# Seven block products for 25 of 32 column-block pairs of the SwiGLU input products, with the sums of weight blocks on GpSimd

## The chip, the core and the metric

The kernel runs on one core of one Trainium2 chip, in one launch. The metric is device time in microseconds; the figure is the median of three runs. All matrices are float32, and TensorE multiplies them as float32r parts: each factor is split into a high part (rounded to float32r) and a low part (what is left), and a product is the sum of three: high by high, low by high, high by low.

## The reference, cut to what matters

256 tokens of 2048 features pass through two layers of three sublayers each. Four of the six sublayers are SwiGLU feed-forward blocks with 4096 hidden features:

```
def swiglu(x, w_in, w_out):                  # x: 256 x 2048, w_in: 2048 x 8192, w_out: 4096 x 2048
    a, gate = jnp.split(x @ w_in, 2, axis=-1)
    return (jax.nn.silu(a) * gate) @ w_out

x = layer_norm(ALPHA * x + 0.5 * swiglu(x, w_in, w_out), g, b)
```

The other two are a stick-breaking attention and a causal pooling mixer. The product `x @ w_in` is what the change is about. Cut into 512 columns, w_in has 8 blocks for `a` and 8 for `gate`; a column-block pair is block n of `a` with block n of `gate`, and there are 8 pairs in each feed-forward block, 32 in all.

## The kernel before

The residual stream lies with features on the partitions: 16 tiles (`xf`) of 128 features by 256 tokens, and beside each its high and low float32r parts (`xs`), side by side.

Weights come from device memory by SyncE's queue in chunks (`chunk`, line 118): four 128-row tiles of 512 columns, 1 MB, into one of three `raw` buffers. For each half of a chunk ScalarE casts the high part into a `whi` tile (line 133) and VectorE subtracts it from the raw weights for the low part, into a `wlo` tile (line 134). Both pools have five tiles of 128x1024.

A product (`gemm`, line 139) goes through the weights a column block at a time. The weights are the stationary operand, 128 columns at a time, and the tokens move: for each 128x128 block of weights the high part meets the 512 columns of [high | low] of x (line 157), the low part meets the 256 columns of the high part (line 160). A column block has 16 row tiles and four 128-column parts, so 64 such couples of products, in four PSUM banks. ScalarE copies the right half of a bank out and VectorE adds the left half (`total`, lines 194 and 195); then come SiLU, the multiplication with the gate (line 334) and the split of the result into parts (line 101).

`ffn_in` (line 319) runs the eight pairs one after the other, `a` block first, then the gate block. In three of the four feed-forward blocks the first pair (in one of them the first two) is computed ahead of the layer norm (`ahead`): x is scaled by the gain only, two columns more carry gain and bias, and all three products go into one sum of 258 columns (lines 151 to 153). Meanwhile the layer norm is finished. GpSimd has nothing to do in these products; it makes constants at the start, takes seven small powers for the layer norms (line 201), and issues eight DMAs at the end.

The last sublayer ends by token: for its output product the tokens are the stationary operand, 128 at a time, and 512 columns of weights move (lines 572 to 574).

The instructions of each engine stand in a fixed order that a scheduler chose when the program was built; an engine starts an instruction when all that stand ahead of it on its queue have been started and its semaphores are there.

Of the kernel before, what the change touches and what calls it, by code (L numbers as in the profile page):

```python
# [13 lines left out]
P = 128  # L14
T = 256
# [20 lines left out]
def trunk(ctx: ExitStack, tc: tile.TileContext, a: dict, out: bass.AP):  # L36
# [4 lines left out]
    whis = ctx.enter_context(tc.tile_pool(name="whis", bufs=5))  # L41
    wlos = ctx.enter_context(tc.tile_pool(name="wlos", bufs=5))
# [24 lines left out]
    # The tensor engine runs at its full clock only after a while of work: products for  # L67
    # nothing, until the first data is here.
# [7 lines left out]
    # tri[k', k] = 1 where k' >= k; past[k, q] = 1 where k < q, twice.  # L76
# [20 lines left out]

    def split(dst, hi_src, lo_src):
# [18 lines left out]
    def chunk(w, r, c, fine=False, step=4):  # L117
        """Four 128-row tiles of 512 columns of w, in halves of hi and lo parts."""
        raw = raws.tile([P, 4, 512], F32, tag="raw", name="raw")
        if fine:  # L120
            for j in range(4):
                load_x(0, j)
                nc.sync.dma_start(raw[:, j], w[r, c, :, j])
        else:
            for j in range(0, 4, step):
                nc.sync.dma_start(raw[:, j:j + step], w[r, c, :, j:j + step])
        his, los = [], []
        for j in range(2):
            hi = whis.tile([P, 2, 512], F32R, tag="whi", name="whi")
            lo = wlos.tile([P, 2, 512], F32R, tag="wlo", name="wlo")  # L130
            for i in ((slice(0, 1), slice(1, 2)) if step < 4 else (slice(0, 2),)):
                src = raw[:, 2 * j:2 * j + 2][:, i]
                nc.scalar.copy(hi[:, i], src)  # L133
                nc.vector.tensor_tensor(out=lo[:, i], in0=src, in1=hi[:, i].bitcast(F32), op=ALU.subtract)  # L134
            his += [hi[:, i] for i in range(2)]
            los += [lo[:, i] for i in range(2)]
        return his, los

    def gemm(w, col, rhs, evac, hooks=None, load=False, one=0, r0=0):
        """Four 128-row tiles of (a 512-column block of w).T @ x, one bank each: hi*hi + lo*hi left,  # L140
        hi*lo right; or all in one sum of that many columns."""
# [41 lines left out]
    def total(dst, ps, norm=None):  # L183
        """dst = left + right half of a product; or, of a raw one, what the layer norm makes of it,
        but for the bias that is returned."""
        if norm is not None:
            aux = tmp.tile([P, 2], F32, tag="aux", bufs=4, name="aux")
            nc.scalar.copy(aux, ps[:, T:W])
            nc.vector.scalar_tensor_tensor(out=dst, in0=norm.rb[:, T:], scalar=aux[:, 0:1], in1=ps[:, :T],
                                           op0=ALU.mult, op1=ALU.add)  # L190
            nc.vector.tensor_tensor(out=dst, in0=dst, in1=norm.rb[:, :T], op=ALU.mult)
            return aux[:, 1:2]
        t = tmp.tile([P, T], F32, tag="half", name="half")
        nc.scalar.copy(t, ps[:, T:])  # L194
        nc.vector.tensor_tensor(out=dst, in0=ps[:, :T], in1=t, op=ALU.add)  # L195

# [9 lines left out]
    class Norm:  # L206
        """LN of what x holds, less a shift: its statistics, 1 / std and -mean on all partitions,
        and its result, for four tiles at a time. Ahead of it, xs = [hi | lo] of gain * x."""
# [12 lines left out]
        def add(self, t):  # L221
            """Tiles t and t + 1."""
            q, j = divmod(t, 4)
            x, s = xq[q][:, j:j + 2].rearrange("p j n -> p (j n)"), self.sums
            if t == 0:
                nc.scalar.copy(s[:, 0], x)
                nc.scalar.activation(s[:, 1], x, AF.Square)
            else:
                sq = tmp.tile([P, 2 * T], F32, tag="sq", name="sq")
# [3 lines left out]
            gx = tmp.tile([P, 2, T], F32, tag="gx", name="gx")  # L233
# [37 lines left out]
    def sublayer_end(w, rhs, factor, gname, bname, hooks=None, one=0):  # L271
        """x <- LN(ALPHA x + factor y): LN of x + (factor / ALPHA) y, with eps / ALPHA**2."""
# [43 lines left out]
    def ffn_in(w_in, norm, hooks=None, npairs=1):  # L316
        gs = [None] * (FF // P)
        for grp in range(FF // 512):
            acts = []
            nm = norm if grp < npairs else None  # L320

            def evac_a(f, ps, acts=acts, nm=nm):
                s = tmp.tile([P, T], F32, tag=f"act{f}", bufs=1, name="act")
# [4 lines left out]
            def evac_gate(f, ps, grp=grp, acts=acts, nm=nm):  # L328
                t = 4 * grp + f
                gs[t] = scratch(t, F32R, f"g{t}").rearrange("p (h n) -> p h n", h=2)  # L330
                g = tmp.tile([P, T], F32, tag="gate", name="gate")
                bias = total(g, ps, nm)
                if bias is None:
                    nc.vector.tensor_tensor(out=g, in0=g, in1=acts[f], op=ALU.mult)
                else:
                    nc.vector.scalar_tensor_tensor(out=g, in0=g, scalar=bias, in1=acts[f], op0=ALU.add, op1=ALU.mult)
                split(gs[t], g, g)

            ca, cg = (w_in, grp, evac_a), (w_in, FF // 512 + grp, evac_gate)
            if nm is not None:  # L340
                ahead(nm, (ca, cg), first=grp == 0, last=grp == npairs - 1)
            else:
                gemm(*ca[:2], whole, ca[2], hooks=(hooks or {}).get(grp), load=grp == 0 and norm is None)
                gemm(*cg[:2], whole, cg[2])
        return gs

    def ffn(p, i, ln, norm, npairs=1):
        gs = ffn_in(a[f'{p}ffn{i}_w_in'], norm, npairs=npairs)
# [5 lines left out]
    def attention(p, norm):  # L354
# [17 lines left out]
        def diag(x):  # L372
            """The two blocks where only some of the keys are past."""
            return x.rearrange("p (j q) -> p j q", j=3)[:, ::2]

        def scores(hg):
            def go():
                hs = range(4 * hg, 4 * hg + 4)
                with tc.manual_schedule(engines={mybir.EngineType.Activation}):
                    for h in hs:  # L380
                        # By key: keys 0..127 for all queries, keys 128..255 for the later queries.
# [8 lines left out]
                    # One table after the other.  # L390
# [4 lines left out]
                for h in hs:  # L395
                    # softplus(z) of the past keys
# [5 lines left out]
        def weights(hg):  # L402
            def go():
# [7 lines left out]
                for h in hs:  # L411
                    # exp(min(log_w, 0))
# [41 lines left out]
    def pooling(p, norm):  # L454
# [3 lines left out]
        gates = {}  # L458

        def evac_u(grp, nm):  # L460
            def evac(f, ps):
# [11 lines left out]
                q = tmp.tile([P, T], F32, tag="sq", name="q")  # L473
# [6 lines left out]
        def evac_g(grp, nm):  # L480
            def evac(f, ps):
                s = tmp.tile([P, T], F32, tag=f"act{f}", bufs=1, name="act")
# [29 lines left out]
    def last(p, norm):  # L512
# [16 lines left out]
        gs = ffn_in(w_in, norm, hooks={2: {0: turn}})  # L529
# [65 lines left out]
    norm = ffn('l0_', 2, 'ln3', norm, npairs=2)  # L595
# [32 lines left out]
```

## Time and profile before

| | |
|---|---|
| Time, median of 3 runs (lowest, highest) | 2683.83 us (2683.7, 2683.9) |
| The profiled execution: span, first to last instruction | 2681.8 us |
| The profiled execution's own time, its span and the 2.0 us by which the median run is longer | 2683.8 us |
| TensorE busy | 2666.7 us (99%) |
| VectorE busy | 1675.7 us (62%) |
| ScalarE busy | 1365.4 us (51%) |
| GpSimd busy | 11.9 us (0%) |
| Granted TensorE clock, mean | 0.998 |
| One plain column-block pair | 44.92 us |

A busy time is the time in which at least one instruction of the engine runs; the mean of one instruction can be longer than its share, since the engines are pipelined and neighbours overlap. What an instruction costs in a row of them is read from the distance of two starts.

### The profile page before, as it was taken

How to read it: one execution, taken by the hardware profiler on the slowest of the kernel's cores; microseconds unless marked ns; L12 is line 12 of the kernel's file. 1: busy time of each engine (PE TensorE's matmuls, PEld its weight loads, DVE VectorE, ACT ScalarE, POOL GpSimd, SP SyncE). 2: the span in 40 equal slices, each digit the busy share in tenths (PEclk: the TensorE clock that was granted, in tenths of full speed). 3: DMA queues.
4: the chain of work that ended last, by engine and by line, in shares of the span. 5: the costliest groups of instructions: out<-in, count | busy, mean ns of one | idle time of the engine just before them, and what ended most of it. 6: DMA issues, size and time to landing. Idle time of an engine off the chain costs nothing.

```text
span 2681.8 us, 38727 instructions
## 1 busy us (share of the span) xinstructions
PE 2666.7 (99%) x15916; PEld 2365.1 (88%) x15916; DVE 1675.7 (62%) x2298; ACT 1365.4 (51%) x1990; POOL 11.9 (0%) x28
## 2 busy tenths in 40 slices
PE   9999999999999999999999999999999999999998
PEld 8888888899999888888988888889888998888886
DVE  6555556585686555565765555667878775555545
ACT  5444444467565444444654444445555565444432
POOL 0000000000000000000000000000000000000000
PEclk9999999999999999999999999999999999999999
DMA  7555555554455555555555555554555545555653
GB/s 255 188 188 187 189 188 189 189 174 162 153 190 183 187 186 186 199 177 201 173 189 189 189 189 189 189 189 170 192 189 176 201 174 182 186 186 187 228 193 126
DMA packets 71521, 499.61 MB, mean 186 GB/s; under 512 B 7984, under 2 KB 8624, under 8 KB 12080
## 3 DMA queue, kind: packets, MB, share of 16 engines
q1 hardware_dynamic: 70704, 495.05, 52.4%
q8 instruction: 124, 2.03, 0.3%
q0 software_dynamic: 640, 2.10, 0.2%
q14 instruction: 53, 0.43, 0.0%
HBM read 495.02 MB, written 2.10 MB: 185 GB/s over the span
## 4 chain that ended last, share of the span: by engine, by line
PE 99%; DVE 1%; DMA 0%; SPq 0%; ACT 0%; issue 0%; DVEq 0%; ACTq 0%
PE ps L157 50%; PE ps L160 26%; PE ps L152 5%; PE ps L151 5%; PE ps L153 5%; PE y L573 2%; PE y L572 2%; PE y L574 2%; PE v L430 1%; PE v L428 1%; PE v L429 1%; DMA xq<-in_x 0%; PE cum L407 0%; DVE z L547 0%; PE bc L257 0%; PE st L244 0%
## 5 line engine op out<-in xcount | busy, mean ns | idle before, releaser
L134 DVE TENSOR_TENSOR wlo<-raw,whi 128x1024 fp32r<-128x1024 f32 (+1 forms) x946 | 1144.3, 1212 | 905.8 <-ACT whi L133 901.2
L133 ACT CAST whi<-raw 128x1024 fp32r<-128x1024 f32 (+1 forms) x946 | 982.0, 1041 | 1080.1 <-PE ps L157 851.9
L157 PE MATMUL ps<-xs,whi 128*128 128x512 f32 x3968 | 1389.8, 396 | 1.1 <-ACT whi L133 0.7
L160 PE MATMUL ps<-xs,wlo 128*128 128x256 f32 x3968 | 1100.5, 280 | 1.0 <-DVE wlo L134 1.0
L157 PEld LDWEIGHTS ps<-xs,whi 128*128 128x128 f32 x3968 | 744.8, 189 | 173.4 <-ACT whi L133 1.0
L160 PEld LDWEIGHTS ps<-xs,wlo 128*128 128x128 f32 x3968 | 748.3, 189 | 7.3 <-DVE wlo L134 1.5
L157 PE MATMUL ps<-g,whi 128*128 128x512 f32 x1536 | 534.9, 394 | 0.0
L160 PE MATMUL ps<-g,wlo 128*128 128x256 f32 x1536 | 427.8, 280 | 0.0
L157 PEld LDWEIGHTS ps<-g,whi 128*128 128x128 f32 x1536 | 287.2, 187 | 65.3
L160 PEld LDWEIGHTS ps<-g,wlo 128*128 128x128 f32 x1536 | 289.7, 189 | 1.1
L152 PE MATMUL ps<-xs,whi 128*128 128x258 f32 (+1 forms) x896 | 252.7, 284 | 0.0
L151 PE MATMUL ps<-xs,whi 128*128 128x258 f32 (+1 forms) x896 | 251.7, 283 | 0.0
L153 PE MATMUL ps<-xs,wlo 128*128 128x258 f32 (+1 forms) x896 | 245.5, 282 | 0.0
L152 PEld LDWEIGHTS ps<-xs,whi 128*128 128x128 f32 x896 | 169.6, 189 | 0.2
L151 PEld LDWEIGHTS ps<-xs,whi 128*128 128x128 f32 x896 | 168.9, 188 | 0.0
L153 PEld LDWEIGHTS ps<-xs,wlo 128*128 128x128 f32 x896 | 167.6, 190 | 0.0
L194 ACT COPY half<-ps 128x256 f32<-128x256 f32 x264 | 97.1, 369 | 121.0 <-PE ps L157 119.6
L572 PE MATMUL y<-wlo,g 128*128 128x512 f32 x256 | 99.6, 389 | 0.0
L573 PE MATMUL y<-whi,g 128*128 128x512 f32 x256 | 99.6, 389 | 0.0
L574 PE MATMUL y<-whi,g 128*128 128x512 f32 x256 | 99.4, 389 | 0.0
L157 PE MATMUL ps<-y,whi 128*128 128x512 f32 x256 | 89.6, 396 | 0.0
L195 DVE TENSOR_TENSOR act<-ps,half 128x256 f32<-128x256 f32 x124 | 52.1, 421 | 46.6 <-ACT half L194 46.6
(151 smaller groups left out, 1677.0 us busy)
## 6 DMA issues: line engine op xcount, KB each, us to landing
raw<-in_l_ffn_w_in SPq DMA_DIRECT2D x252, 1024.0 KB, 4.8
raw<-in_l_ffn_w_out SPq DMA_DIRECT2D x127, 1024.0 KB, 4.8
raw<-in_l_pool_w_in SPq DMA_DIRECT2D x32, 1024.0 KB, 4.9
raw<-in_l_sb_w_qkv SPq DMA_DIRECT2D x24, 1024.0 KB, 4.8
raw<-in_l_pool_w_out SPq DMA_DIRECT2D x16, 1024.0 KB, 4.9
raw<-in_l_sb_w_o SPq DMA_DIRECT2D x8, 1024.0 KB, 4.9
raw<-in_l_pool_w_grp SPq DMA_DIRECT2D x4, 1024.0 KB, 4.9
raw<-in_l_ffn_w_in SPq DMA_DIRECT2D x6, 512.0 KB, 9.4
```

The lines of the kernel that those rows point to most:

```text
L133: nc.scalar.copy(hi[:, i], src)
L134: nc.vector.tensor_tensor(out=lo[:, i], in0=src, in1=hi[:, i].bitcast(F32), op=ALU.subtract)
L151: nc.tensor.matmul(ps[:, :one], hi[:, cs], x[:, 0, :one], start=first, stop=False)
L152: nc.tensor.matmul(ps[:, :one], hi[:, cs], x[:, 1, :one], start=False, stop=False)
L153: nc.tensor.matmul(ps[:, :one], lo[:, cs], x[:, 0, :one], start=False, stop=last)
L157: nc.tensor.matmul(ps.rearrange("p (h n) -> p h n", h=2), hi[:, cs], x, start=first, stop=last)
L160: nc.tensor.matmul(ps[:, :T], lo[:, cs], x[:, 0], start=False, stop=False)
L194: nc.scalar.copy(t, ps[:, T:])
L195: nc.vector.tensor_tensor(out=dst, in0=ps[:, :T], in1=t, op=ALU.add)
L572: nc.tensor.matmul(ps[m], gh, lo, start=kk == 0, stop=False)
L573: nc.tensor.matmul(ps[m], gl, hi, start=False, stop=False)
L574: nc.tensor.matmul(ps[m], gh, hi, start=False, stop=kk == nk - 1)
```

## The change

A column-block pair becomes one 2x2 block product. The tokens are cut into two blocks of 128 and the 2048 features into two of 1024, so x is [A11 A12; A21 A22]; the weights of the pair are [B11 B12; B21 B22], where the first index is the half of the features and the second is `a` or `gate`. Eight block products of 128 tokens by 1024 features by 512 columns are replaced by seven (Winograd's form of Strassen's product). The four sums of x blocks are made once per feed-forward block on GpSimd (`prepare`). The four sums of weight blocks are made for each 128 features of both halves, eight times in a pair, on GpSimd (`ta`: B12-B11 and B12-B22; `tb`: B22 less the first of these, and B21 less that). High and low parts of B11, of B21 and B22, of `ta` and of `tb` are then made on ScalarE and VectorE as before. In the seven products the tokens are stationary and 512 columns of weights move.

25 of the 32 pairs go this way. In the first feed-forward block the first pair stays as it was. In the other three the first pair is computed ahead of the layer norm as before, and the second by a plain product with the tokens stationary (`gemm_x`). In the feed-forward block that had two pairs ahead of the layer norm, one is left.

The results of the pairs by `gemm_x` and by seven products lie by token. They are multiplied, turned by TensorE's transposes to lie by feature, kept in float32 (`whole_pair`), and split into parts later (`settle`): eight tiles within the last pair, 24 behind it. Buffers: `whi` and `wlo` have six tiles, two tiles for the sums are new, and several small tiles share a pool (`wide`). The host lays out the weights of the 25 pairs by blocks; it adds nothing up.

```
+    sums = ctx.enter_context(tc.tile_pool(name="sums", bufs=2))
-    whis = ctx.enter_context(tc.tile_pool(name="whis", bufs=5))
-    wlos = ctx.enter_context(tc.tile_pool(name="wlos", bufs=5))
+    whis = ctx.enter_context(tc.tile_pool(name="whis", bufs=6))
+    wlos = ctx.enter_context(tc.tile_pool(name="wlos", bufs=6))
...
+    def gemm_x(w, col, rhs):
...
+                for m in range(2):
+                    xh, xl = (rhs[kk][:, h, m * P:(m + 1) * P] for h in range(2))
+                    nc.tensor.matmul(ps[m], xh, his[k], start=kk == 0, stop=False)
+                    nc.tensor.matmul(ps[m], xl, his[k], start=False, stop=False)
+                    nc.tensor.matmul(ps[m], xh, los[k], start=False, stop=kk == nk - 1)
+        return ps
+    class Seven:
...
+        def prepare(self, q):
+            a11, a21 = (xq[q][:, :, m * P:(m + 1) * P] for m in range(2))
+            a12, a22 = (xq[q + 2][:, :, m * P:(m + 1) * P] for m in range(2))
+            t = [wide(f"s{i}").rearrange("p (j n) -> p j n", j=4) for i in range(4)]
+            for dst, x, y, op in ((t[0], a21, a22, ALU.add), (t[1], t[0], a11, ALU.subtract),
+                                  (t[3], a12, t[1], ALU.subtract), (t[2], a21, a11, ALU.subtract)):
+                nc.gpsimd.tensor_tensor(out=dst, in0=x, in1=y, op=op)
...
+        def run(self, w, grp, hooks):
...
+            for i in range(8):
+                raw = raws.tile([P, 4, 512], F32, tag="raw", name="raw")
+                nc.sync.dma_start(raw, w[grp, i])
+                b11, b2, b22, b21 = raw[:, 1], raw[:, 2:4], raw[:, 3], raw[:, 2]
+                def parts(hi, lo, src):
+                    nc.scalar.copy(hi, src)
+                    nc.vector.tensor_tensor(out=lo, in0=src, in1=hi.bitcast(F32), op=ALU.subtract)
...
+                ta, tb = (sums.tile([P, 2, 512], F32, tag="sum", name=n) for n in ("ta", "tb"))
+                nc.gpsimd.tensor_tensor(out=ta, in0=raw[:, 0:1].to_broadcast([P, 2, 512]), in1=raw[:, 1:4:2],
+                                        op=ALU.subtract)
+                nc.gpsimd.tensor_tensor(out=tb[:, 0], in0=b22, in1=ta[:, 0], op=ALU.subtract)
+                nc.gpsimd.tensor_tensor(out=tb[:, 1], in0=b21, in1=tb[:, 0], op=ALU.subtract)
...
+                parts(h11, l11, b11)
+                hb, lb = pair()
+                parts(hb, lb, b2)
+                ha, la = pair()
+                parts(ha, la, ta)
+                ht, lt = pair()
+                parts(ht, lt, tb)
...
+                for n in ((1, 2, 6, 5, 3, 7, 4) if i == 7 else products):
+                    (xh, xl), hi, lo = products[n]
...
+                    nc.tensor.matmul(p, xh, hi, start=i == 0, stop=False)
+                    nc.tensor.matmul(p, xl, hi, start=False, stop=False)
+                    nc.tensor.matmul(p, xh, lo, start=False, stop=i == 7)
...
+            nc.scalar.copy(s1, p1)
+            add(c11, p2, s1)
+            add(u2, p6, s1)
+            add(u4, p5, u2)
+            add(c12, p3, u4)
+            add(c22, p7, u4)
+            add(u2, p7, u2)
+            add(c21, p4, u2)
+            return (c11, c21), (c12, c22)
...
+        def settle(ts):
+            for t in ts:
...
+                split(gs[t], src, src)
...
+        def gated(grp, a, g):
+            for m in range(2):
+                nc.vector.tensor_tensor(out=a[m], in0=a[m], in1=g[m], op=ALU.mult)
...
+                            nc.tensor.transpose(ps[:, j * T + m * P:j * T + (m + 1) * P], a[m][:, f * P:(f + 1) * P],
+                                                ident)
+                    nc.scalar.copy(whole_pair(2 * grp + h), ps)
...
+        seven.prepare(0)
+        seven.prepare(1)
+        late = None
+        for grp in range(1, std):
+            pa = gemm_x(w_in, grp, xs)
...
+        for grp in range(std, ng):
+            hs = {1: late} if late else {}
+            if grp == ng - 1:
+                hs[5] = lambda: settle(range(8))
+            acts, gates = seven.run(w_seven, grp - std, hs)
+            late = gated(grp, silu(acts, acts), gates)
+        late()
+        settle(range(8, 32))
         return gs
```

What this makes of the engines' queues is seen at two places. The first is GpSimd's queue. Before, this is all that it holds between the start of the program and its end: a counter and two masks, five powers of a variance (`var`), and at the end the DMAs of a gain (`gb`).

```order
L88 IOTA count_115 128x16
L79 AFFINE_SELECT tri_107<-tri_107 128x128
L85 AFFINE_SELECT past_112<-past_112 128x256
L201 TENSOR_TENSOR rn_4979<-var_4983,mhalf_105 128x2
L201 TENSOR_TENSOR rn_7104<-var_7108,mhalf_105 128x2
...
L534 DMA gb0_23347<-in_l1_ln3_g 128x512 x4
```

Now, in the middle of the pairs by seven products of the first feed-forward block, it stands like this (`raw` is the chunk of weights, `ta` and `tb` the sums):

```order
L379 TENSOR_TENSOR tb_842<-raw_839,ta_841 128x512
L380 TENSOR_TENSOR tb_842<-raw_839,tb_842 128x512
L377 TENSOR_TENSOR ta_883<-raw_881 128x1024
L379 TENSOR_TENSOR tb_884<-raw_881,ta_883 128x512
L380 TENSOR_TENSOR tb_884<-raw_881,tb_884 128x512
L377 TENSOR_TENSOR ta_927<-raw_925 128x1024
L379 TENSOR_TENSOR tb_928<-raw_925,ta_927 128x512
L380 TENSOR_TENSOR tb_928<-raw_925,tb_928 128x512
```

Three subtractions of weight blocks for each 1 MB of weights are added, 600 in all, and 32 sums of x blocks beside them; the powers stay.

The second place is VectorE's queue within the first feed-forward block. Before, around the evacuation of a gate block (`ps`, `half`), it holds the low parts of the weights, two for each chunk, and the small tiles of the activations:

```order
L134 TENSOR_TENSOR wlo_1372<-raw_1369,whi_1371 128x1024
L134 TENSOR_TENSOR wlo_1376<-raw_1369,whi_1375 128x1024
L134 TENSOR_TENSOR wlo_1418<-raw_1415,whi_1417 128x1024
L195 TENSOR_TENSOR gate_1314<-ps0_1175,half_1315 128x256
L334 TENSOR_TENSOR gate_1314<-gate_1314,act_1121 128x256
L195 TENSOR_TENSOR gate_1330<-ps1_1176,half_1331 128x256
L334 TENSOR_TENSOR gate_1330<-gate_1330,act_1134 128x256
L101 TENSOR_TENSOR g8_1313<-gate_1314,g8_1313 128x256
```

Now, at the end of a pair by seven products (`p2`, `p6`: PSUM banks of two of the products; `su` and `c11`: sums of products; `half` and `act` are gone):

```order
L369 TENSOR_TENSOR wlo_2042<-raw_2030,whi_2041 128x1024
L369 TENSOR_TENSOR wlo_2038<-raw_2074,whi_2037 128x512
L369 TENSOR_TENSOR wlo_2046<-ta_2032,whi_2045 128x1024
L369 TENSOR_TENSOR wlo_2050<-tb_2033,whi_2049 128x1024
L369 TENSOR_TENSOR wlo_2084<-raw_2074,whi_2083 128x1024
L418 TENSOR_TENSOR c11_2118<-p2_1778,su_2116 128x512
L369 TENSOR_TENSOR wlo_2088<-ta_2076,whi_2087 128x1024
L369 TENSOR_TENSOR wlo_2092<-tb_2077,whi_2091 128x1024
L369 TENSOR_TENSOR wlo_2142<-raw_2134,whi_2141 128x512
L369 TENSOR_TENSOR wlo_2146<-raw_2134,whi_2145 128x1024
L418 TENSOR_TENSOR su_2116<-p6_1794,su_2116 128x512
```

For each 1 MB of weights VectorE now holds three and a half subtractions of 1024 elements instead of two, half of their elements made by GpSimd (`ta`, `tb`), and the sums of products stand between those of the next pair's first weights (`raw_2134`).

## Rows read from the trace of the kernel before

**Rows 1.** The page: busy us of each engine, share of the span, instructions.

```profile
PE 2666.7 (99%) x15916; PEld 2365.1 (88%) x15916; DVE 1675.7 (62%) x2298; ACT 1365.4 (51%) x1990; POOL 11.9 (0%) x28
```

**Rows 2.** The page: the chain that ended last, shares of the span by engine.

```profile
PE 99%; DVE 1%; DMA 0%; SPq 0%; ACT 0%; issue 0%; DVEq 0%; ACTq 0%
```

**Rows 3.** Windows: a plain pair; 192 matmuls by token of the last output product.

```profile
core 0: us, PE busy (x) PEld busy (x) DVE busy (x) ACT busy (x) POOL busy (x), PEclk, DMA share, GB/s
1385.12:1430.04 44.92, 44.92 (x258) 39.20 (x257) 25.37 (x34) 22.12 (x33) 0.00 (x0) 1.00 0.53 187
2538.90:2582.30 43.40, 43.40 (x194) 35.92 (x193) 22.09 (x20) 16.76 (x17) 0.00 (x0) 1.00 0.55 194
```

**Rows 4.** Waits of the whole run: in total, times, longest.

```profile
engine line waited for: us in total, times, longest us
DVE wlo L134 <- ACT whi L133: 901.2, 667, 5.1
ACT whi L133 <- PE ps L157: 851.9, 562, 4.2
```

**Rows 5.** Timeline, VectorE: low parts back to back (us of the start, us).

```profile
start us, us, engine line op out<-in xcount [idle before <-releaser]
14.02 2.56 DVE L134 TENSOR_TENSOR wlo<-raw,whi 128x512 fp32r<-128x512 f32 x4
27.77 2.36 DVE L134 TENSOR_TENSOR wlo<-raw,whi 128x1024 fp32r<-128x1024 f32 x2 [3.08 <-ACT whi L133]
```

**Rows 6.** Groups by form, VectorE: names, shapes, count, busy us, mean ns.

```profile
L134 DVE TENSOR_TENSOR wlo<-raw,whi 128x1024 fp32r<-128x1024 f32 x926 | 1131.2, 1223 | 898.9 <-ACT whi L133 894.6
L588 DVE SCALAR_TENSOR_TENSOR z<-y,z 128x512 f32<-128x512 f32 x8 | 5.5, 687 | 6.5 <-PE y L574 6.5
L101 DVE TENSOR_TENSOR g<-gate,g 128x256 fp32r<-128x256 f32 x128 | 53.0, 418 | 0.0
```

**Rows 7.** Groups by form, ScalarE: the high parts.

```profile
L133 ACT CAST whi<-raw 128x1024 fp32r<-128x1024 f32 x926 | 970.4, 1050 | 1071.9 <-PE ps L157 851.9 <-PE y L574 93.8 <-PE ps L152 91.8
```

**Rows 8.** Groups by form, GpSimd: the powers and two masks.

```profile
L201 POOL TENSOR_TENSOR rn<-var,mhalf 128x2 f32<-128x2 f32 x5 | 3.5, 695 | 2138.4 <-DVE var L251 2138.4
L201 POOL TENSOR_TENSOR rs<-ve,mhalf 128x1 f32<-128x1 f32 x2 | 1.9, 968 | 184.8 <-DVE ve L542 184.8
L85 POOL TENSOR_SCALAR_AFFINE_SELECT past<-past 128x256 f32<-128x256 f32 x1 | 0.4, 396 | 0.0
L79 POOL TENSOR_SCALAR_AFFINE_SELECT tri<-tri 128x128 f32<-128x128 f32 x1 | 0.3, 282 | 0.0
```

**Rows 9.** Timeline, GpSimd: one of five early powers, and the last two.

```profile
561.57 0.71 POOL L201 TENSOR_TENSOR rn<-var,mhalf 128x2 f32<-128x2 f32 x1 [558.94 <-DVE var L251]
2665.69 1.00 POOL L201 TENSOR_TENSOR rs<-ve,mhalf 128x1 f32<-128x1 f32 x1 [178.67 <-DVE ve L542]
2672.85 0.93 POOL L201 TENSOR_TENSOR rs<-ve,mhalf 128x1 f32<-128x1 f32 x1 [6.16 <-DVE ve L542]
```

**Rows 10.** Timeline, VectorE: beside these three powers.

```profile
561.33 0.15 DVE L251 SCALAR_TENSOR_TENSOR var<-st,m 128x2 f32<-128x2 f32 x1
563.98 1.23 DVE L134 TENSOR_TENSOR wlo<-raw,whi 128x1024 fp32r<-128x1024 f32 x1 [2.50 <-ACT whi L133]
2665.52 1.41 DVE L547 SCALAR_TENSOR_TENSOR z<-z,mv,gb 128x512 f32<-128x512 f32 x2
2666.84 0.75 DVE L552 SCALAR_TENSOR_TENSOR z<-z,rs,gb 128x512 f32<-128x512 f32 x1
2672.63 1.40 DVE L547 SCALAR_TENSOR_TENSOR z<-z,mv,gb 128x512 f32<-128x512 f32 x2
2673.95 0.74 DVE L552 SCALAR_TENSOR_TENSOR z<-z,rs,gb 128x512 f32<-128x512 f32 x1
```

**Rows 11.** The page: DMA issues of input weights, median us to landing.

```profile
raw<-in_l_ffn_w_in SPq DMA_DIRECT2D x252, 1024.0 KB, 4.8
```

**Rows 12.** The chain in order of time: eight 128-column float32 matmuls.

```profile
565.85 0.89 PE bc L257 x8
```

More of the change, by code (lines that the diff above doesn't have):

```diff
@@ L96, in vec, with wide @@
         return vecs[:, c:c + 1]
+    def wide(name):
+        return tmp.tile([P, 512], F32, tag="wide", bufs=4, name=name)
     def split(dst, hi_src, lo_src):
@@ L313, in ahead @@
             gemm(w, col, xs, evac, hooks=hooks, one=W)
-    def ffn_in(w_in, norm, hooks=None, npairs=1):
-        gs = [None] * (FF // P)
[L318 to L323, printed above, removed]
+    def gemm_x(w, col, rhs):
+        nk = len(rhs)
+        ps = [bank(f"px{m}") for m in range(2)]
+        for c in range(nk // 4):
+            his, los = chunk(w, c, col)
+            for k in range(4):
+                kk = 4 * c + k
+                for m in range(2):
[4 more added lines that the diff above has]
+        return ps
@@ new lines, in ffn_in, with whole_pair, silu, go @@
+    def ffn_in(w_in, w_seven, norm, hooks=None):
+        ng = FF // 512
+        ahead_of = 0 if norm is None else 1
+        std = ahead_of + 1 if norm is not None else 1
+        g32 = [None] * (FF // P // 2)
+        gs = [None] * (FF // P)
+        seven = Seven()
+        def whole_pair(i):
+            g32[i] = scratch(i, F32, f"gw{i}")
+            return g32[i]
+        def settle(ts):
+            for t in ts:
+                slot = 16 + t if t < 16 else 32 if t == 31 else t - 16
+                gs[t] = scratch(slot, F32R, f"g{t}").rearrange("p (h n) -> p h n", h=2)
+                src = g32[t // 2][:, t % 2 * T:(t % 2 + 1) * T]
+                split(gs[t], src, src)
+        def silu(a, src):
+            for m in range(2):
+                nc.scalar.activation(a[m], src[m], AF.Silu)
+            return a
+        def gated(grp, a, g):
+            for m in range(2):
+                nc.vector.tensor_tensor(out=a[m], in0=a[m], in1=g[m], op=ALU.mult)
+            def go():
+                for h in range(2):
+                    ps = bank("gt")
+                    for j in range(2):
+                        f = 2 * h + j
+                        for m in range(2):
+                            nc.tensor.transpose(ps[:, j * T + m * P:j * T + (m + 1) * P], a[m][:, f * P:(f + 1) * P],
+                                                ident)
+                    nc.scalar.copy(whole_pair(2 * grp + h), ps)
+            return go
+        def by_feature(grp):
+            acts, pairs = [], []
+            nm = norm
+            def evac_a(f, ps):
+                if f % 2 == 0:
+                    pairs.append(wide("act"))
+                s = pairs[-1][:, f % 2 * T:(f % 2 + 1) * T]
@@ L333, in evac_gate @@
                 if bias is None:
-                    nc.vector.tensor_tensor(out=g, in0=g, in1=acts[f], op=ALU.mult)
+                    nc.vector.tensor_tensor(out=dst, in0=g, in1=acts[f], op=ALU.mult)
                 else:
[L336 to L344, printed above, removed]
@@ L345, in ffn_in @@
-        return gs
-    def ffn(p, i, ln, norm, npairs=1):
-        gs = ffn_in(a[f'{p}ffn{i}_w_in'], norm, npairs=npairs)
+                    nc.vector.scalar_tensor_tensor(out=dst, in0=g, scalar=bias, in1=acts[f], op0=ALU.add, op1=ALU.mult)
+            return (w_in, 0, evac_a), (w_in, std, evac_gate)
+        ca, cg = by_feature(0)
+        if norm is not None:
+            ahead(norm, (ca, cg))
+        else:
+            gemm(*ca[:2], whole, ca[2], load=True)
+            gemm(*cg[:2], whole, cg[2])
@@ new lines, in ffn_in @@
+        seven.prepare(0)
[3 more added lines that the diff above has]
+            pa = gemm_x(w_in, grp, xs)
+            acts = silu([wide(f"a{m}") for m in range(2)], pa)
+            if hooks:
+                hooks()
+            late = gated(grp, acts, gemm_x(w_in, std + grp, xs))
+        for grp in range(std, ng):
[4 more added lines that the diff above has]
+            late = gated(grp, silu(acts, acts), gates)
@@ L349, in ffn @@
+        late()
+        settle(range(8, 32))
+        return gs
+    def ffn(p, i, ln, norm):
+        gs = ffn_in(a[f'{p}ffn{i}_w_in'], a[f'{p}ffn{i}_w_in_seven'], norm)
         if norm is None:
@@ L457, in pooling @@
                       for i, n in enumerate(("y", "po")))
-        gates = {}
+        gates, pairs = {}, []
         def evac_u(grp, nm):
@@ L527, in turn @@
                     nc.scalar.copy(z[q][:, m, :], ps[m])
-        gs = ffn_in(w_in, norm, hooks={2: {0: turn}})
+        gs = ffn_in(w_in, a[f'{p}ffn2_w_in_seven'], norm, hooks=turn)
         for i, name in enumerate((f'{p}ln3_g', f'{p}ln3_b')):
@@ L594, in trunk @@
     norm = attention('l0_', norm)
-    norm = ffn('l0_', 2, 'ln3', norm, npairs=2)
+    norm = ffn('l0_', 2, 'ln3', norm)
     norm = ffn('l1_', 1, 'ln1', norm)
@@ L614 @@
             value = value[0].T.reshape(4, 4, P, T).transpose(0, 2, 1, 3)
+        elif name.endswith('_w_in') and '_ffn' in name:
+            std = 1 if name == 'l0_ffn1_w_in' else 2
+            blocks = value.reshape(2, 8, P, 2, 8, 512)
+            laid[name + '_seven'] = np.stack(
+                [blocks[h, :, :, n, std:] for h, n in ((0, 1), (0, 0), (1, 0), (1, 1))]).transpose(3, 1, 2, 0, 4)
+            value = blocks[:, :, :, :, :std].reshape(4, 4, P, 2 * std, 512).transpose(0, 3, 2, 1, 4)
         elif '_w_' in name:
```

57 lines of the change are left out of this document (49 added, 8 removed).

## The prediction

> **What bounds the kernel now.** I read the page's busy times first: TensorE 99%, VectorE 62%, ScalarE 51%, GpSimd nothing [rows 1]. The chain that ended last says the same, 99% TensorE [rows 2]. Then windows over one column-block pair: it takes 44.92 us, TensorE is busy in all of it at the full granted clock, and VectorE in 25.37 us, ScalarE in 22.12 us [rows 3]. The waits confirm the direction: VectorE's low parts wait for ScalarE's high parts, and those for TensorE to give buffers back [rows 4]. So the input products are bound by TensorE, and work taken from it is worth its time until another engine becomes the limit. The question is which engine comes next, since the change takes a little from TensorE and gives much to VectorE and GpSimd.
>
> **TensorE's part.** A pair had 128 products of 512 columns and 128 of 256 in 44.92 us. By seven products it has 7 x 8 x 3 = 168 of 512 columns with the tokens stationary. The last output product is of that form: 192 in 43.40 us, so 0.226 us each [rows 3]. 168 x 0.226 = 38.0 us, and eight transposes of 128 columns at 0.89 / 8 = 0.11 us [rows 12] make 38.9 us. TensorE alone would give back 6.0 us for each of 25 pairs, 150 us. Each of the three pairs by `gemm_x` is 192 such products, 43.4 instead of 44.9 us (taking a pair ahead of the norm at the plain price): 5 us together.
>
> **VectorE's part.** In a pair there are eight steps of 1 MB. In each the low parts are three subtractions of 1024 elements and one of 512 where there were two of 1024. Back to back, four of 512 took 2.56 us and two of 1024 took 2.36 [rows 5]; less one whole duration (0.69 for a VectorE operation on 512 and 1.22, [rows 6]) that is a distance of 0.62 and 1.14 us. A step is 3 x 1.14 + 0.62 = 4.04 us, eight are 32.3. At the pair's end come seven sums from PSUM and two gate products of 512, 9 x 0.62 = 5.6 us; together 37.9 us, just under TensorE. ScalarE's 1024-element cast is 1.05 us [rows 7]: three and a half in a step, 8 x 3.7 = 29.4 us, not a limit.
>
> **GpSimd's part.** A step adds one subtraction of 1024 and two of 512, in a chain: `tb` needs `ta`, its second half needs its first. No row of before shows a GpSimd operation on two large inputs. The nearest are the masks with one input, 0.282 us for 128 elements and 0.396 for 256 [rows 8]: 0.89 ns an element and 0.17 us fixed. If two inputs cost no more than one, a step's 2048 elements cost 2048 x 0.89 + 3 x 0.17 = 2.3 us; if two reads and a write each cost that in turn, 6.0 us. I take two reads, 4.15 us. Alone, beside the others, that is 33 us a pair and hidden.
>
> [...]
>
> **Whether the two run side by side.** This decides the sign. All of VectorE's low parts read two tensors from SBUF, and so does every one of the new GpSimd instructions. The trace has seven small GpSimd operations with two inputs. The five powers for the layer norms fell where VectorE was idle: at 561.57 us VectorE had just ended at 561.48 and next started at 563.98. They took 0.695 us in the mean. The two at the end started 0.17 and 0.22 us after a VectorE operation with two SBUF inputs (line 547) and took 1.00 and 0.93 us, with fewer elements [rows 8 to 10]. The first of each couple on line 547 gives way to the second 0.66 us after its start, at 2666.18 and 2673.29; the powers ended at 2666.69 and 2673.78, 0.51 and 0.49 us behind that change in both cases, whenever they had started. I read this as GpSimd's read having waited until VectorE's operation was through. It would be 0.23 to 0.31 us of waiting for a tiny operation; I carry 0.27 us as the price of a change between the two engines. What the rows don't show is the reverse, VectorE waiting for a long GpSimd instruction, since the powers read one element.
>
> [...]
>
> **The sum, if they exclude each other.** A step is VectorE's 4.04 us, GpSimd's 4.15 and three changes at 0.27: 9.0 us, twice TensorE's 168 x 0.226 / 8 = 4.75. A step's 1 MB lands in 4.8 us [rows 11] and is covered. There is always one side ready: while ScalarE casts `ta`, VectorE has the raw blocks' low parts; while it casts `tb`, GpSimd can start the next `ta`. Behind a low part that waits stand the sums that free PSUM banks, and TensorE waits for those. Eight steps are 72.0 us. The gate products, with both inputs in SBUF, add 1.2; of the seven sums from PSUM (4.3 us), which leave the second input's path to GpSimd, I take half, 2.2. A pair is 75.4 us, 30.5 more than before; 25 pairs give +762.
>
> Smaller terms: `prepare` has eight GpSimd operations of 512 and eight low parts, which in the first feed-forward block stand right ahead of the first step: I estimate +8, since half of its 8 x 1.08 lies beside the first pair's own work and the rest returns as exclusion in the other three. At each block's end the last sums, the gate product and the transposes stand in a row, some five VectorE operations of 0.62, 3 us each: +12. The 24 splits behind them, at most 24 x 0.42 = 10 us [rows 6], are hidden by the output product on the first eight tiles, already split: 32 couples at 44.92 / 128, 11 us. `gemm_x`: -5. Sum +777 on the profiled execution, whose span of 2681.8 and 2.0 around it are the median of 2683.8: **3460 us**.
>
> With GpSimd at 2.3 us and changes free, a step is 6.4 and a pair 52.2: +183, some 2880. At 6.0 it is 10.8, a pair 92: +1180, 3880. Since two inputs need two reads, I take 3250 to 3750 as this case's own range. If waiting lets TensorE's granted clock fall to half, its 21 products in a step take 9.5 us, a little over the 9.0, and add up to 100; the clock was 1.00 in all windows of before that I use [rows 3], so this is a bound, not a term.
>
> **The rivals.**
> Exclusion in part: they share the path so that GpSimd reads in VectorE's gaps. A step costs some 7.0 us, between 4.04 + 2.3 and 9.0; a pair 59, +360, 3060. For it: VectorE's pair on line 547 was not stretched (1.41 us for two). Against it: a one-element read could not have stretched it.
> No exclusion, faster: the two late powers were longer for another reason, their shape say. Then TensorE's 38.9, VectorE's 37.9 and GpSimd's 33 us run side by side. They meet at the pair's end, where TensorE waits for banks; I take 1.6 us. 40.5 us a pair, -4.4 x 25 = -110, with the small terms 2590. It decides as soon as GpSimd's and VectorE's times don't add up. For it: the five undisturbed powers say nothing of contention. Against it: the two that were disturbed ended at the same distance from VectorE's change.
> GpSimd alone as the limit, without exclusion, at 6.0 us a step: 48 us a pair, +77 and some waiting, about 2790.
> That the change makes the counts it says is plain from the queues; nothing of it is left out by the scheduler.
>
> **How the numbers follow.** Exclusion 0.62, in part 0.17, no exclusion 0.16, GpSimd alone 0.03, a balance at no change 0.02. A run of this kernel can tell 0.2% from nothing, 5.4 us. Faster 0.16, the same 0.02, slower 0.82. The range from 2780 to 3750 leaves out the faster case and a tail of the slowest, 2 in 10.
>
> **What would show it.** Right: 7 to 10 us a step; VectorE's low parts or GpSimd's subtractions waiting for each other, as longer durations or as gaps; TensorE's share down to about 73%, with waits for low parts; GpSimd busy some 800 us or more. Wrong: a pair at 39 to 42 us, TensorE still near 99%; or subtractions of 1024 on GpSimd that take 3 us with VectorE undisturbed. It would be wrong in size if GpSimd's operation differs from 4.15 us a step: each 0.1 us is 20 us.

## The result, and the profile after

The changed kernel takes 3353.49 us (3351.27 to 3354.99, 4 runs) against 2683.76 us before (4 runs): 1.2495 times the time, 95% interval 1.2477 to 1.2513. It is 669.7 us slower; 776 had been forecast.

The page after (busy times; then GpSimd and the granted TensorE clock in 40 slices) answers to [rows 1]:

```profile
PE 2812.4 (84%) x13620; PEld 2215.4 (66%) x13620; DVE 2732.3 (82%) x2617; ACT 1632.1 (49%) x2223; POOL 1399.1 (42%) x660
...
POOL 4777773000017777720067777400000057777300
PEclk9999898999999999989999989799999999999799
```

TensorE went from 99% to 84%, VectorE from 62% to 82%, GpSimd from nothing to 42%, in four stretches: the pairs by seven products. The window of one such pair, from the first `ta` of a pair to that of the next, answers to the first line of [rows 3]:

```profile
core 0: us, PE busy (x) PEld busy (x) DVE busy (x) ACT busy (x) POOL busy (x), PEclk, DMA share, GB/s
261.00:331.00 70.00, 49.51 (x177) 33.12 (x177) 64.77 (x42) 31.17 (x38) 52.44 (x25) 0.95 0.34 121
```

A pair takes 70.0 us where it took 44.92. VectorE is busy in 64.8 of it and GpSimd in 52.4, together 117 us in 70, though the work of both was reckoned at 38 and 33. Where the surplus comes from is seen in the groups by form, three of GpSimd and four of VectorE (count, busy us, mean ns of one):

```profile
L377 POOL TENSOR_TENSOR ta<-raw 128x1024 f32<-128x1024 f32 x200 | 570.2, 2851 | 326.8 <-DVE wlo L369 295.0 <-DMA raw<-in_l_ffn_w_in_seven 31.8
L379 POOL TENSOR_TENSOR tb<-raw,ta 128x512 f32<-128x512 f32 x200 | 353.6, 1768 | 140.3 <-DVE wlo L369 133.0
L380 POOL TENSOR_TENSOR tb<-raw,tb 128x512 f32<-128x512 f32 x200 | 383.1, 1916 | 15.6
...
L369 DVE TENSOR_TENSOR wlo<-raw,whi 128x1024 fp32r<-128x1024 f32 x200 | 529.0, 2645 | 2.9 <-ACT whi L368 2.9
L369 DVE TENSOR_TENSOR wlo<-ta,whi 128x1024 fp32r<-128x1024 f32 x200 | 314.1, 1570 | 6.9 <-ACT whi L368 5.4
L369 DVE TENSOR_TENSOR wlo<-tb,whi 128x1024 fp32r<-128x1024 f32 x200 | 382.6, 1913 | 107.3 <-ACT whi L368 106.8
L369 DVE TENSOR_TENSOR wlo<-raw,whi 128x512 fp32r<-128x512 f32 x200 | 273.1, 1368 | 3.9 <-ACT whi L368 3.9
```

A low part of 1024 elements took 1.22 us before [rows 6]; here the means are 1.57 to 2.65. GpSimd's subtraction of 1024 took 2.38 us in the mean of 94 of its 200 executions (none of these over 2.45), and 3.3 us or more in the slowest quarter. Both engines are shown as "busy" while they wait for each other. Who waits for whom stands in the timeline (start, duration), first GpSimd, then VectorE in the same stretch:

```profile
200.17 2.36 POOL L377 TENSOR_TENSOR ta<-raw 128x1024 f32<-128x1024 f32 x1 [1.77 <-DVE wlo L369]
203.76 1.28 POOL L379 TENSOR_TENSOR tb<-raw,ta 128x512 f32<-128x512 f32 x1 [1.22 <-DVE wlo L369]
205.12 1.30 POOL L380 TENSOR_TENSOR tb<-raw,tb 128x512 f32<-128x512 f32 x1
```

```profile
200.01 0.68 DVE L418 TENSOR_TENSOR u<-p,su 128x512 f32<-128x512 f32 x1
200.61 3.00 DVE L369 TENSOR_TENSOR wlo<-tb,whi 128x1024 fp32r<-128x1024 f32 x1
203.53 1.28 DVE L418 TENSOR_TENSOR c<-p,u 128x512 f32<-128x512 f32 x2
205.33 2.16 DVE L369 TENSOR_TENSOR wlo<-raw,whi 128x1024 fp32r<-128x1024 f32 x1
```

The low part of `tb` starts at 200.61 while GpSimd makes `ta`, which ends at 202.53; the low part ends at 203.61, 1.08 us behind. That is about what a whole low part takes in a row of them (1.14 us, [rows 5]), so I take it that it had not begun to read. The same at 205.33: GpSimd ends at 206.42, VectorE at 207.49. Between them VectorE's two sums that read a PSUM bank (203.53, 1.28 us for two, line 418) lie beside GpSimd's `tb` (203.76, 1.28 us) and neither is stretched. Of the 506 low parts of 1024 that stand alone in a row of the timeline, 268 took longer than 1.3 us, and every one of them ended 1.07 to 1.10 us behind the end of a GpSimd instruction.

GpSimd waits in the same way. Here VectorE's low part started first and ended at 290.10, and `ta`, which started meanwhile, ended at 292.36, 2.26 us behind it; alone it takes 2.38:

```profile
288.89 1.21 DVE L369 TENSOR_TENSOR wlo<-tb,whi 128x1024 fp32r<-128x1024 f32 x1
289.05 3.31 POOL L377 TENSOR_TENSOR ta<-raw 128x1024 f32<-128x1024 f32 x1 [2.37 <-DVE wlo L369]
```

Of the 106 executions of `ta` that took over 2.45 us, 90 ended 2.22 to 2.28 us behind the end of such a VectorE instruction.

The waits (in total, times, longest) show what hangs on it, where [rows 4] had TensorE as the one that others waited for:

```profile
ACT whi L368 <- POOL tb L380: 544.5, 186, 4.3
PE p L408 <- DVE wlo L369: 365.1, 409, 2.7
POOL ta L377 <- DVE wlo L369: 295.0, 144, 4.4
PE gt L467 <- DVE c L459: 46.2, 4, 12.4
```

The last line is another matter: four waits of TensorE at the ends of the feed-forward blocks, three of some 12 us and one of 10.

### The profile page after: what moved, and what is told of

The parts are those of the page before. It is cut to its first block, busy times and chain, and to the rows that moved or that the text cites. A ratio compares the mean times of both kernels' runs of the same rounds, so it can differ in the third digit from the quotient of the medians.

```text
span 3352.1 us, 36377 instructions
## 1 busy us (share of the span) xinstructions
PE 2812.4 (84%) x13620; PEld 2215.4 (66%) x13620; DVE 2732.3 (82%) x2617; ACT 1632.1 (49%) x2223; POOL 1399.1 (42%) x660
## 5 line engine op out<-in xcount | busy, mean ns | idle before, releaser
L138 DVE TENSOR_TENSOR wlo<-raw,whi 128x1024 fp32r<-128x1024 f32 (+1 forms) x546 | 664.3, 1223 | 430.3 <-ACT whi L137 429.8
L137 ACT CAST whi<-raw 128x1024 fp32r<-128x1024 f32 (+1 forms) x546 | 558.1, 1033 | 557.8 <-PE ps L161 354.2
L369 DVE TENSOR_TENSOR wlo<-raw,whi 128x512 fp32r<-128x512 f32 (+1 forms) x400 | 789.1, 2007 | 6.9 <-ACT whi L368 6.8
L377 POOL TENSOR_TENSOR ta<-raw 128x1024 f32<-128x1024 f32 x200 | 570.2, 2851 | 326.8 <-DVE wlo L369 295.0
L408 PE MATMUL p<-wlo,s 128*128 128x512 f32 x800 | 337.4, 456 | 186.0 <-DVE wlo L369 183.5
L369 DVE TENSOR_TENSOR wlo<-tb,whi 128x1024 fp32r<-128x1024 f32 x200 | 382.6, 1913 | 107.3 <-ACT whi L368 106.8
L406 PE MATMUL p<-whi,s 128*128 128x512 f32 x800 | 349.0, 436 | 107.5 <-ACT whi L368 83.5
L379 POOL TENSOR_TENSOR tb<-raw,ta 128x512 f32<-128x512 f32 x200 | 353.6, 1768 | 140.3 <-DVE wlo L369 133.0
L380 POOL TENSOR_TENSOR tb<-raw,tb 128x512 f32<-128x512 f32 x200 | 383.1, 1916 | 15.6
L407 PE MATMUL p<-whi,s 128*128 128x512 f32 x800 | 335.1, 419 | 0.0
L369 DVE TENSOR_TENSOR wlo<-ta,whi 128x1024 fp32r<-128x1024 f32 x200 | 314.1, 1570 | 6.9 <-ACT whi L368 5.4
```

The lines of the kernel that those rows point to most:

```text
L377: nc.gpsimd.tensor_tensor(out=ta, in0=raw[:, 0:1].to_broadcast([P, 2, 512]), in1=raw[:, 1:4:2], op=ALU.subtract)
L379: nc.gpsimd.tensor_tensor(out=tb[:, 0], in0=b22, in1=ta[:, 0], op=ALU.subtract)
L380: nc.gpsimd.tensor_tensor(out=tb[:, 1], in0=b21, in1=tb[:, 0], op=ALU.subtract)
L406: nc.tensor.matmul(p, xh, hi, start=i == 0, stop=False)
L407: nc.tensor.matmul(p, xl, hi, start=False, stop=False)
L408: nc.tensor.matmul(p, xh, lo, start=False, stop=i == 7)
```

## The experiments

All are edits of the changed kernel. Times are medians; "before" beside them was 2683.6 to 2683.7 us on the same chip.

**Without the sums.** The raw blocks stand in for the sums.

```
-                ta, tb = (sums.tile([P, 2, 512], F32, tag="sum", name=n) for n in ("ta", "tb"))
-                nc.gpsimd.tensor_tensor(...)   # three
+                ta, tb = raw[:, 0:2], raw[:, 2:4]
```

> The three GpSimd subtractions of each step are left out, and the raw blocks stand in for the sums; everything else of the changed kernel stays. Theory (VectorE and GpSimd exclude each other): a pair falls from 70.0 us to TensorE's 38.9 or VectorE's 37.9 us plus one or two at its end, the time to about 2600 us (2560 to 2660). Rival A (the chain GpSimd, ScalarE, VectorE through two sum buffers is too long, each of them undisturbed): the same here, the two are told apart by the runs with another operand. Rival B (the seven products themselves don't run at 0.226 us, for waits on banks or a granted clock at half): the time stays above 2900 us.

Measured: 2618.59 us, 0.9758 of before (0.9729 to 0.9786). That is within the range of the theory. All else of the change is thus worth -65 us and the three GpSimd instructions, with all that waits for them, cost 735. Rival B is out: in the middle of the pairs TensorE is busy throughout, at the full granted clock, as this window shows.

```profile
180.00:220.00 40.00, 40.00 (x179) 32.50 (x179) 37.88 (x42) 31.38 (x37) 0.00 (x0) 1.00 0.61 210
```

The run doesn't say yet how the three instructions cost their time.

**Second operand in SBUF or in PSUM.** Two kernels that differ in where a constant lies that the low part subtracts (and in its value, 1.0 in SBUF and 0.001 in PSUM); both leave out the split into true low parts and the transposes at a pair's end.

```
-                    nc.vector.tensor_tensor(out=lo, in0=src, in1=hi.bitcast(F32), op=ALU.subtract)
+                    nc.vector.tensor_tensor(out=o, in0=x, in1=y, op=ALU.subtract)
     # o, x: lo and src in runs of 128; y: 128 columns, repeated, of `ones` in SBUF
     # or of a tile in an eighth PSUM bank of its own
```

> Control for the next run. In the pairs by seven products the low part is the weights less a constant that lies in SBUF, in place of the high part; the transposes at a pair's end are left out (the tiles are copied as they lie), and PSUM has seven banks for products. VectorE still has two inputs from SBUF, but no longer waits for ScalarE. Theory (exclusion): 3250 to 3360 us, since the sum of VectorE's and GpSimd's time stays. Rival A (long chain): clearly faster, 3000 to 3200 us, since one link of the chain is gone.

> As the control, but the constant that the low part subtracts lies in PSUM: VectorE has one input from SBUF, and all else is the same. Theory (exclusion by the second SBUF input): the two engines run side by side, a pair falls to GpSimd's 8 x 4.92 = 39.4 us undisturbed plus 2 to 5, the time to 2620 to 2730 us, and GpSimd's subtraction of 1024 takes 2.4 us throughout. Rival A (long chain), and a rival by which any work of VectorE disturbs GpSimd: within 2% of the control.

Measured: 3284.87 us with the constant in SBUF (1.2241 of before, 1.2205 to 1.2276), 2663.28 us in PSUM (0.9924, 0.9896 to 0.9953). Groups by form of the one in SBUF, one of GpSimd and two of VectorE:

```profile
L384 POOL TENSOR_TENSOR ta<-raw 128x1024 f32<-128x1024 f32 x200 | 554.2, 2771 | 292.7 <-ACT whi L369 181.9 <-ACT c L460 64.1 <-DMA raw<-in_l_ffn_w_in_seven 31.3
...
L376 DVE TENSOR_TENSOR wlo<-raw,ones 128x1024 fp32r<-128x1024 f32 x200 | 500.8, 2504 | 2.0 <-PE px L333 2.0
L376 DVE TENSOR_TENSOR wlo<-tb,ones 128x1024 fp32r<-128x1024 f32 x200 | 425.6, 2128 | 47.6 <-POOL tb L387 44.2 <-issue 1.9 <-PE px L333 1.6
```

and of the one in PSUM:

```profile
L386 POOL TENSOR_TENSOR ta<-raw 128x1024 f32<-128x1024 f32 x200 | 499.9, 2500 | 96.8 <-ACT whi L371 46.9 <-DMA raw<-in_l_ffn_w_in_seven 31.1 <-ACT gw L472 10.3
...
L378 DVE TENSOR_TENSOR wlo<-raw,small 128x1024 fp32r<-128x1024 f32 x200 | 242.6, 1213 | 6.5 <-PE px L335 6.4
L378 DVE TENSOR_TENSOR wlo<-tb,small 128x1024 fp32r<-128x1024 f32 x200 | 243.2, 1216 | 97.7 <-POOL tb L389 91.7 <-PE px L335 4.7 <-issue 1.0
```

The same VectorE instructions by count and size, the same GpSimd work, and 622 us between them. With one input in SBUF VectorE's low part is 1.21 us and GpSimd's `ta` 2.50; a pair in the middle of a block is 42.9 us, where GpSimd's own 8 x (2.41 + 1.30 + 1.29) = 40.0 us is the longest part. Rival A expected the control to be much faster, as it waits for no cast, and the two to agree. Both failed: the control is 601 us slower than before, 24.0 us for each of the 25 pairs if all of it lies there, where a pair of the changed kernel takes 25.1 us more than before. So here it was VectorE's second input from SBUF that excluded.

**GpSimd that writes but doesn't read, and that reads one input.** The sums are left out in both.

```
-                nc.gpsimd.tensor_tensor(...)   # three
+                nc.gpsimd.memset(ta, 0.5)      # and the halves of tb
```

> The three GpSimd subtractions of each step become memsets of the same tiles, so GpSimd writes and doesn't read; the sums are left out by that. By the rows of before a memset costs 0.11 us and 0.76 ns an element: 0.88, 0.50 and 0.50 us, 1.9 us a step. If only reads exclude: VectorE's low parts keep 1.22 us and the time is that of the run without sums, within 1%. If writes exclude as well: a step is 4.04 + 1.9 us, a pair some 50.8, the time about 2870 us.

```
-                nc.gpsimd.tensor_tensor(...)   # three
+                nc.gpsimd.tensor_copy(out=ta, in_=raw[:, 1:4:2])   # and the halves of tb from b22, b21
```

> The three GpSimd subtractions of each step become copies of the same sizes, one input from SBUF in place of two; the sums are left out by that. By the masks' rows of before (0.17 us and 0.89 ns an element) the three are 1.08, 0.62 and 0.62 us, 2.3 us a step. If any GpSimd read excludes a VectorE operation with two SBUF inputs: a step is 4.04 + 2.3 less the 0.3 that the changed kernel's turns overlap, some 6.0 us, a pair 50 to 52, the time 2850 to 2910 us, and VectorE's low parts are stretched beside the copies. If it takes two inputs on both sides: the time of the run with memsets, 2626 us, and low parts of 1.22 us throughout.

Measured: 2626.51 us with memsets (0.9787 of before, 0.9759 to 0.9816), 2891.64 us with copies (1.0775, 1.0753 to 1.0797). The groups with memsets:

```profile
L377 POOL MEMSET ta<- 128x1024 f32 x200 | 191.3, 957 | 572.5 <-DVE wlo L369 572.5
...
L369 DVE TENSOR_TENSOR wlo<-raw,whi 128x1024 fp32r<-128x1024 f32 x200 | 243.7, 1218 | 13.2 <-ACT whi L368 12.5
```

and with copies:

```profile
L377 POOL COPY ta<-raw 128x1024 f32<-128x1024 f32 x200 | 267.0, 1335 | 319.2 <-DVE wlo L369 288.0 <-DMA raw<-in_l_ffn_w_in_seven 31.2
...
L369 DVE TENSOR_TENSOR wlo<-raw,whi 128x1024 fp32r<-128x1024 f32 x200 | 313.9, 1570 | 13.3 <-ACT whi L368 13.3
```

Beside memsets of 0.96 us a low part is as long as before (1.22 us) and the time is 0.3% above that without sums; beside copies, of which a `ta` takes 1.04 us when undisturbed, it has a mean of 1.57. A pair with copies is 50.5 to 51.5 us in the middle of a block. The GpSimd instruction that only wrote excluded nothing here (1.22 us); one input read was enough (1.57).

**The sums on VectorE.**

```
-                nc.gpsimd.tensor_tensor(out=ta, ...)   # and the two of tb
+                nc.vector.tensor_tensor(out=ta, ...)
```

> The sums of weight blocks stay, with the same result, but VectorE makes them, so nothing runs on GpSimd within a pair. Theory (exclusion): the two engines took turns anyway, so the time goes by the sum of one engine's work: 4.04 + 1.14 + 2 x 0.62 = 6.4 us a step in place of 8.6, a pair 51.4 + 5.6 = 57 us, 25 x 12.1 = +302, and the 43 us more than 25 pairs that the changed kernel has over the kernel before: about 3030 us (2980 to 3060). Faster than with GpSimd, slower than before. Rival (the GpSimd work was partly hidden): VectorE's load grows by 2.4 us a step and the time is no shorter than the changed kernel's 3353.

Measured: 3029.68 us, 1.1289 of before (1.1269 to 1.131). The three sums there:

```profile
L377 DVE TENSOR_TENSOR ta<-raw 128x1024 f32<-128x1024 f32 x200 | 244.3, 1222 | 4.3 <-DMA raw<-in_l_ffn_w_in_seven 4.1
L379 DVE TENSOR_TENSOR tb<-raw,ta 128x512 f32<-128x512 f32 x200 | 136.6, 683 | 0.2
L380 DVE TENSOR_TENSOR tb<-raw,tb 128x512 f32<-128x512 f32 x200 | 136.8, 684 | 0.9
```

They cost VectorE 1.22 + 2 x 0.68 us a step where GpSimd took 4.9 and held VectorE up for it: work that was moved to an idle engine is 324 us cheaper on the loaded one.

**The other part of the change alone.** All pairs but the first of each block by `gemm_x`, no seven products.

```
-        std = ahead_of + 1 if norm is not None else 1
+        std = ng
...
+            settle(range(4 * grp - 4, 4 * grp))
```

> The other part of the change alone: the seven products are left out, and all pairs but the first of each feed-forward block go by gemm_x (192 products of 512 columns with the tokens stationary), then transposes and late splits, the splits of a pair within the next one. By the trace 43.4 us and 0.9 us of transposes stand against 44.92: -0.6 us for 28 pairs, -17, and some 2 us at each block's end for the last gate product and transposes that TensorE waits for: 2670 to 2680 us, 0.2 to 0.5% faster than before. Rival (waits at the transposes or for banks in each pair): the same or up to 1% slower.

Measured: 2698.25 us, 1.0054 of before (1.004 to 1.0067): 0.5% slower, so this expectation failed, and its cause was a price. Two products of line 330, the one ten rounds of three products behind the other (start, duration):

```profile
100.21 0.39 PE L330 MATMUL px<-whi,xs 128*128 128x512 f32 x1
107.18 0.40 PE L330 MATMUL px<-whi,xs 128*128 128x512 f32 x1
```

30 products from 100.21 to 107.18, 6.97 us, are 0.232 us each, not the 0.226 of the last output product. 192 x 0.232 + 0.9 = 45.5 us against 44.92: +0.6 for 28 pairs, +16, and +14.5 was measured. Why the one form has 0.226 and the other 0.232 wasn't tried.

**The end of a block.** The transposes and late splits behind the first chunks of the output product; nothing is left out.

```
-        late()
-        settle(range(8, 32))
-        return gs
+        def rest():
+            late()
+            settle(range(28, 32))
+        return gs, {0: lambda: settle(range(8, 28)), 1: rest}   # hooks of the output product's chunks
```

> The changed kernel with one thing moved: at the end of each feed-forward block the 20 splits of tiles 8 to 27 stand behind the first chunk of the output product, and the last pair's transposes and the last four splits behind the second chunk, in place of all of them ahead of the product. The result is the same. Theory: in the changed kernel TensorE waits in four places for the last gate product, 46.2 us in all, because the transposes stand ahead of the output product on its queue, and VectorE has five low parts and twelve splits ahead of that gate product; two chunks are 11 us of work that needs neither. So 25 to 45 us go, 3308 to 3330 us. Rival (the wait only moves to the first product that needs the late tiles, or to the low parts of the output weights): within 10 us of 3353.

Measured: 3296.97 us, 1.2286 of before (1.2266 to 1.2307), 56 us less than the changed kernel, rather more than the 25 to 45 expected. Of the waits at the transposes this is left:

```profile
PEld gt L467 <- DVE c L459: 5.0, 12, 0.4
```

What stood in the way in the changed kernel is seen in its timeline of VectorE at the end of the first block: six low parts of the output weights (`wlo` of line 138) and eight splits (line 105) between the pair's own last low part and the gate product (line 459).

```profile
546.36 1.21 DVE L369 TENSOR_TENSOR wlo<-tb,whi 128x1024 fp32r<-128x1024 f32 x1
547.49 1.21 DVE L138 TENSOR_TENSOR wlo<-raw,whi 128x1024 fp32r<-128x1024 f32 x1
...
549.23 2.34 DVE L138 TENSOR_TENSOR wlo<-raw,whi 128x1024 fp32r<-128x1024 f32 x2
...
552.10 1.21 DVE L138 TENSOR_TENSOR wlo<-raw,whi 128x1024 fp32r<-128x1024 f32 x1
553.23 1.75 DVE L105 TENSOR_TENSOR g<-gw,g 128x256 fp32r<-128x256 f32 x5
...
556.70 2.34 DVE L138 TENSOR_TENSOR wlo<-raw,whi 128x1024 fp32r<-128x1024 f32 x2
558.97 1.08 DVE L105 TENSOR_TENSOR g<-gw,g 128x256 fp32r<-128x256 f32 x3
559.98 0.68 DVE L459 TENSOR_TENSOR c<-c,c 128x512 f32<-128x512 f32 x1
```

The rows left out are the sums of products. TensorE's transposes stood ahead of the output product:

```profile
560.80 0.45 PE L467 MATMUL gt<-ident,c 128*128 128x128 f32 x1 [11.96 <-DVE c L459]
```

The wait has a second price. The granted clock fell to 0.50 while TensorE waited (1.00 from 549 to 552 us, 0.50 from 555 to 561), and the output product began at that. The window of the changed kernel right behind the wait and one further on:

```profile
561.00:565.00 4.00, 4.00 (x14) 3.52 (x14) 1.61 (x4) 0.63 (x1) 0.00 (x0) 0.50 0.55 229
580.00:600.00 20.00, 20.00 (x115) 17.34 (x115) 8.79 (x8) 7.34 (x7) 0.00 (x0) 1.00 0.54 197
```

At the four ends this lasted 3 to 5 us, 17 in all, in which half of the work was done: I estimate 8 us. With the 46.2 of waiting that is most of the 56 us.

No kernel of these that computes the whole beats the kernel before: the form that runs in 2618 us has no sums, the one in 2663 no low parts. Nor are these two times bounds on what the seven products could give here, since the first still has the waits at the blocks' ends:

```profile
PE gt L463 <- DVE c L455: 57.8, 4, 14.5
```

The version without sums and with the blocks' ends moved was not run.

## Why the prediction was right, and where its sizes were off

- TensorE as the bound before, and no longer after: right. Without the sums the time is 2.4% under before, so TensorE did give time back, and it is the limit again there.
- The price of a product of that form, 0.226 us from the last output product: too low for `gemm_x`, which has 0.232. It bears on the faster rival and not on the forecast.
- VectorE's low parts at 1.14 and 0.62 us: right. The run with the sums on VectorE, worked out from these distances and the 43 us outside the pairs, came out at 3030 as expected.
- GpSimd's 4.15 us a step: too low. Undisturbed it is 2.38 + 1.28 + 1.29 = 4.95 us. That made the step 0.8 us too short, 160 us over the 200 steps.
- That the two engines take turns: right, and now shown from both sides by the pair of operands. Two SBUF inputs on VectorE gave 3285 us and one gave 2663; beside a GpSimd instruction that doesn't read SBUF the time was 2627 us, beside one that reads a single input 2892; and VectorE waited for whole instructions (268 of 268 low parts). Before the runs no row showed VectorE waiting for a long GpSimd instruction: that was my estimate from the two late powers.
- 0.27 us for each change between the engines: wrong in sign. VectorE's 4.04 and GpSimd's 4.95 make 8.99 us a step, 72 a pair, and a whole pair with its end took 70.0. The turns overlap a little: a low part that was held ended 1.08 us behind GpSimd's instruction and takes 1.21 alone, a held `ta` 2.25 behind VectorE's and takes 2.38, so 0.13 us less each time. The three changes at 0.27 made the step 0.8 us too long, as much as GpSimd's price had made it too short. That the step came out at 9.0 us in the forecast is luck: two errors of some 160 us each cancelled. What is left, with the sums from PSUM, half of which I counted, made the pair 75.4 us in the forecast; 5.4 x 25 = 135 us too much. That those sums leave GpSimd's way free, and the half of 2.2 us, no row of before showed; in the timeline above two of them take 1.28 us beside a `tb` of 1.28, and with the constant in PSUM a low part takes 1.21 us beside a `ta` of 2.50.
- The block's end at 3 us each, 12 in all: the term that was furthest off for its size. TensorE waited 46.2 us in four places, since the last gate product stood behind low parts and splits on VectorE's queue and the transposes ahead of the output product on TensorE's. Moving them gave 56 us back. All that lies outside the 25 pairs cost 669.7 - 25 x 25.1 = 42 us, forecast 15. So the forecast of 3460 us was 107 too high because 135 too much within the pairs stands against 27 too little outside them.
- The granted clock: it was 0.952 in the mean, with stretches at 0.50 within the pairs (one from 262.0 to 265.4 us), where TensorE waits for low parts (365.1 us in all). With VectorE and GpSimd as the limit I see no sign that it cost time within the pairs: the control with the constant in SBUF has a mean of 0.936 and is no slower (3285 us against 3353). No run separates it. At the blocks' ends, where TensorE is the limit, it did cost some 8 us by the estimate above, and the prediction had no term for that.
- The signs: the step at 8.75 us (70.0 / 8), the long low parts and GpSimd's 1399 us (waiting included) are as foretold. TensorE's share is 84% and not 73%: it is busy 2812 us, where the run without sums, with the same products, has 2546.
- Two of the sums for other prices don't come out of their own terms. With 2.3 us on GpSimd and free changes a step is 6.3 and a pair 54 us, so some 2930 us and not 2880; with 6.0 a pair is 90 and not 92, some 3830 us and not 3880. The forecast doesn't use them.

## What to carry to other kernels

GpSimd was idle before, and work moved to it was not free: with all that waited for it, it cost 735 us. Before moving elementwise work to GpSimd, count how many inputs from SBUF the VectorE instructions beside it have. With two, the times of both added up here (70.0 us a pair), and that was longer than VectorE took for all of the work alone (57 us a pair, worked out from the 3029.68 us of that run less the 43 outside the pairs); with one of them in PSUM (42.9 us a pair), or with GpSimd only writing (2626.51 us for the whole, 0.3% above the run without sums), they ran side by side. Work on a queue at the seam of two stages was priced here by what stood ahead of it on that queue (46.2 us of waiting in four places, forecast as 12), not by its own length, and a wait of TensorE there cost a slow start behind it as well (3 to 5 us at a granted clock of 0.50). Two errors in a sum can cancel: check a forecast by its terms, not by its total.

## What I had not expected of the hardware

A GpSimd copy with a single input, of 1.04 us, held up VectorE's two-input operations as a subtraction did (a mean of 1.57 us for 1.22). VectorE's operations with one input from PSUM and one from SBUF ran beside GpSimd's two-input subtraction with nothing to see on either (1.28 us for two of them and 1.28 us for `tb`, in the timeline above). And 512-column products with the tokens stationary had two rates in otherwise like stretches (granted clock 1.00 in the window of the last output product, 0.999 in the mean of the run by `gemm_x`), 0.226 and 0.232 us.
